# FFN 1's down projection: first four mixer weight tiles split by casting transfers, root table and gain rescale sooner, one low part by an adding transfer

## The chip, the cores and the metric

The kernel runs as one program on one core of a Trainium2 chip. The metric is the device time of one execution in microseconds (us). A core has five engines with instruction queues of their own, each worked off in order: TensorE (PE, matrix products), VectorE (DVE), ScalarE (ACT), GpSimd (POOL) and SyncE (SP, which here only issues transfers). POOL also issues transfers, among them those that add into their destination or change the element type on the way. Transfers run on 16 DMA engines that all queues share. Engines wait for each other by semaphores.

## The reference

One layer of a streaming encoder trunk on 512 tokens of width 1024, in float32:

```
h = x + 0.5 * post1(SwiGLU_1(pre1(x)))            # FFN 1, hidden width 2816
u = pre_mix(h)
[q | k | v | x_rnn | x_gate] = u @ w_in           # the mixer
... RG-LRU branch, windowed attention, gates, merge
h = h + post_mix(merged @ w_o)
y = h + 0.5 * post2(SwiGLU_2(pre2(h)))            # FFN 2
SwiGLU(x) = (silu(x @ w1) * (x @ w3)) @ w2
```

`pre`, `post` and `pre_mix` are root-mean-square norms with a gain vector. The change lies where `@ w2` of FFN 1 ends, its norms `post1` and `pre_mix` are taken, and the first products of the mixer (`x_rnn`, called `xr`) begin.

## The kernel before

**Precision.** Every float32 product is made of three faster ones. An operand is split into a high part (a float32r rounding, names `whi`, `hx`, `Xh`) and a low part (what is left, `wlo`, `hx`, `Xl`), and high by high, high by low and low by high are summed in PSUM. The usual split (`split2`, L226 and L227) is an ACT copy into float32r for the high part and a DVE subtraction for the low one. `split_dma` does without DVE: ACT writes the high part, ACT writes the negated source into the low part, and a POOL transfer adds the source from DRAM to it.

**w2 of FFN 1 by halves.** `Halves` multiplies the hidden activations by `w2` with a scheme of seven products per block pair instead of eight (`m1`, `m5`, `m2`, `m6`, `m3`, `m7`, `m4`, in this order). The inner dimension is cut into six groups (`GS_A`, the last of them half as large), so there are 42 units, numbered u = 0 to 41: product number u // 6, group u % 6. One unit is 12 matmuls of 512 columns (6 in the half group), for two token tiles, into the two PSUM banks of its product (`hw`). `m1`, `m6`, `m7` and `m4` add up in the same banks `bu`, one per token tile: after `m6` and `m7` the partial sums are read out (`out`, into `hc`), and the next product goes on adding on top. So the first `m4` matmul into a bank may not start before the `m7` sum of this bank has been read: that read is the DVE addition at L742.

**What sets the order.** The code is written in the order in which the instructions stand in each queue. `step(u)` first prepares operands up to unit u + 5 (`prep`, two `split2` each: the weight block, then the activations), then runs the hooks of u, then the matmuls. `tok_gemm` with `pre` strings them together: units 0 to 29, `norm(0)` of token tile 0 (rows and `h` by DVE and ACT in turns, L308 to L346), preparation of units 38 and 39, units 30 to 33, units 34 and 35 for tile 0, then for tile 1, `norm(1)`, units 36 to 41 for tile 0, transposes, and so on. `vectors` at u = 18 has POOL load the two gain vectors into all partitions (`bcast`, L294: `bc_ffn1_post_g`, `bc_mix_pre_g`); a hook at u = 24 has ACT rescale the second of them (L438), and a hook at u = 26 has ACT run a tiny reciprocal root so that the root's function table is loaded there (L437).

**The mixer's first tiles.** At u = 26, 28, 31 and 33 (`X_AT`) the raw weight tiles `xr` 0 to 3 are loaded by SP. They are split by `dma_split`, in two parts: part 0 is the ACT high part, part 1 the ACT negated copy and the adding transfer of POOL. Tile 0 is split ahead of `norm(0)`, tile 1 in its middle (`mid`, which stands between the two ACT root steps of a norm), tile 2 ahead of `norm(1)`, tile 3's high part in its middle and its low part after the second transposes.

**Slots.** All large tiles come from one pool of 42 slots of 4 KB per partition. A transfer or an instruction that takes a slot waits until the last reader of the slot's former tile is done.

Of the kernel before, what the change touches and what calls it, by code (L numbers as in the profile page):

```python
# [11 lines left out]
F32R = mybir.dt.float32r  # L12
AF = mybir.ActivationFunctionType
ALU = mybir.AluOpType

P = 128
# [35 lines left out]
def hybrid_layer(ctx: ExitStack, tc: tile.TileContext, a: dict, out: bass.AP):  # L52
# [18 lines left out]
    def small(w, name="m", bufs=4):  # L71
        uid[0] += 1
        return sm.tile([P, w], F32, tag=f"sm{w}", name=f"{name}_{uid[0]}", bufs={1: 11, 4: 12}.get(w, bufs))
# [61 lines left out]
    want("w2b", TAIL_B)  # L135

    st = {"dma": 0, "split": 0, "get": 0}
    raws, pairs, half_split = {}, {}, {}

    loaded = set()  # L140

    def dma_one(k):
        if k not in loaded:
            nm, i = order[k]
            raws[k] = slot([P, D], name=f"raw_{nm}{i}")
            sp.dma_start(out=raws[k], in_=a[nm][i * P : (i + 1) * P, :])
            loaded.add(k)

    def dma_to(n):
        while st["dma"] < min(n, len(order)):  # L150
            dma_one(st["dma"])
            st["dma"] += 1
# [8 lines left out]
        pool.dma_start(out=lo, in_=src, accum_op=ALU.add)  # L161
        return hi, lo

    def dma_split(k, part):
        assert k == st["split"]
        if part == 0:
            dma_to(k + 1)
            half_split[k] = slot([P, D], F32R, name="whi"), slot([P, D], F32R, name="wlo")
            act.activation(half_split[k][0], raws[k], AF.Copy)
            return  # L170
        pairs[k] = hi, lo = half_split.pop(k)
        act.activation(lo, raws.pop(k), AF.Copy, scale=-1.0)
        nm, i = order[k]
        pool.dma_start(out=lo, in_=a[nm][i * P : (i + 1) * P, :], accum_op=ALU.add)
        st["split"] += 1
# [202 lines left out]
    def tok_gemm(nm, xs, n, R, gpost_name, scale, gpre_name, first, x_to=None, xf=None, spill=False, then=None, eps=None, pre=None):  # L378
# [52 lines left out]
        def norm(t, mid=None):  # L431
            us[t] = norms(acc[t], t, g[0], scale, g[1], spill, ep(t), mid, pre and pre.part(t), (1, 0) if pre and t > 1 else (0, 1))

        if pre:
            G = pre.G
            pre.hooks[3 * G].append(vectors)
            pre.hooks[4 * G + 2].append(lambda: act.activation(small(1, "tiny"), veps[:, 0:1], AF.Abs_reciprocal_sqrt))  # L437
            pre.hooks[4 * G].append(lambda: act.activation(g[1], g[1], AF.Copy, scale=NEWT))  # L438
            x0 = st["get"] + len(tail)
            for i, u in enumerate(X_AT):  # L440
                pre.hooks[u].append(lambda i=i: dma_to(x0 + i + 1))

            def x_split(i, parts=(0, 1)):
                for p in parts:
                    dma_split(x0 + i, p)

            for u in range(5 * G):
                pre.step(u)
            for t in range(2):
                acc[t] = [pre.bank["bc"][t], pre.bank["bx"][t]]  # L450
            pre.prep(5 * G + LEAD + 3)
            x_split(0)
            norm(0, lambda: x_split(1))
            pre.prep(7 * G - 2)
            for u in range(5 * G, 6 * G - 2):
                pre.step(u)
            for t in range(2):
                for u in range(6 * G - 2, 6 * G):
                    pre.step(u, (t,))
                if t == 0:  # L460
                    pre.prep(7 * G)
            for t in range(2, 4):
                acc[t] = [pre.bank["bu"][t - 2], None]
            pre.hid.eo.clear()
            x_split(2)
            norm(1, lambda: x_split(3, (0,)))
            for u in range(6 * G, 7 * G):
                pre.step(u, (0,))
            trs[0] = transpose_mm(us[0])
            transpose_out(trs[0], 0)  # L470
            for u in range(6 * G, 6 * G + 2):
                pre.step(u, (1,))
            trs[1] = transpose_mm(us[1])
            transpose_out(trs[1], 1)
            x_split(3, (1,))
            norm(2, lambda: [transpose_xf(trs[0], 0, xf), transpose_xf(trs[1], 1, xf, (0,))])
            transpose_xf(trs[1], 1, xf, (1,))
            for u in range(6 * G + 2, 7 * G):
                pre.step(u, (1,))
            pre.bank.clear()  # L480
        else:
# [121 lines left out]
    class Halves:  # L603
# [84 lines left out]
        def prep(self, n, load=True):  # L688

            G = self.G  # L690
            while self.ready < min(n, self.cap):
                u = self.ready
                self.ready += 1
                m, i = self.names[u // G], u % G
                J = len(self.gs[i])
                if load:
                    self.load(max(G, u))
                b, odd, half = self.OPERANDS[m]
                hi = slot([P, 2, 512], F32R, name="whi")
                if J == 2:  # L700
                    lo = slot([P, 2, 512], F32R, name="wlo")
                else:
                    hi, lo = hi[:, 0:1, :], hi[:, 1:2, :]
                if u < U_SLOTS or u >= self.in_slots:
                    xs = slot([P, 2, 2, 256], F32R, name="hx")
                else:
                    xs = uT[:, :, (u + 1) % 8, :].rearrange("p e (j c) -> p e j c", j=2)
                src = self.again.pop(i) if m == "m3" else self.raw[b, i]
                split2(hi, lo, src)
                split2(xs[:, 0, :J, :], xs[:, 1, :J, :], self.x(i, odd, half))  # L710
                self.ops[u] = hi, lo, xs
                if self.again_at <= u < self.again_at + G:
                    n = u - self.again_at
                    self.again[n] = slot([P, 2, 512], name=f"raw_{self.nm}")[:, : len(self.gs[n]), :]
                    sp.dma_start(out=self.again[n], in_=self.src("b22", n))
                self.sums(m, i)
# [1133 lines left out]
GRAW_AT = (29, 30)  # L1850
TB_AT = (34, 35, 36, 37)

BY_DMA = {("wg", i) for i in range(2)} | {("xr", i) for i in range(4)}

BY_POOL = {("wg", i) for i in range(2, 8)} | {("wk", 0), ("wk", 1)}

TAIL_A = ()
LEAD = 5
# [72 lines left out]
```

## Time and profile before

| | us |
|---|---|
| runs shown (3) | 1104.5, 1101.29, 1103.9; median 1103.9 |
| the profiled execution, its own time | 1103.1 |
| its span, first to last instruction | 1100.9 |
| PE busy in the span | 1089.4 (99%) |
| DVE busy | 937.1 (85%) |
| ACT busy | 711.2 (65%) |
| POOL busy | 423.8 (38%) |

Times inside the execution are counted from the span's start. A row of the timeline reads: start, duration, engine, line, operation, output <- input, shapes, count; in brackets at its end the idle time of the engine just before it and what ended it. Durations of ACT and DVE overlap a little: the next instruction starts about 0.1 us before the one before it is listed as ended. PE matmuls are pipelined; what counts there is the distance between starts (0.227 us for 512 columns at full clock). Tile names are printed without buffer numbers, so the group's `bc_ffn1_post_g` reads `bc_ffn_post_g`. The end of FFN 1's `w2` that the change touches lies between 280 and 355 us.

### The profile page before, as it was taken

To read this page: it belongs to the slowest core of one execution; us is meant where nothing else is said; L and a number is where in the kernel's file an instruction comes from. 1 tells how busy PE (TensorE), PEld (TensorE's weight loads), DVE (VectorE), ACT (ScalarE), POOL (GpSimd) and SP (SyncE) were. 2 spreads that over 40 slices of the span, in tenths; PEclk is the share of its full clock that TensorE was granted. 3 is DMA by queue.
4 is the path that set the end of the run, shared out by engine and by line. 5 is a ranking of instruction groups with operands and counts; after the bars stand their busy time and mean duration, and the time that the engine had idled before them with its cause. 6 is when DMAs were issued, how large, how long until landed. Compare 5 with 4: busy or idle time off the path is not lost.

```text
span 1100.9 us, 18128 instructions
## 1 busy us (share of the span) xinstructions
PE 1089.4 (99%) x6850; PEld 986.1 (90%) x6850; DVE 937.1 (85%) x1347; ACT 711.2 (65%) x1243; POOL 423.8 (38%) x351
## 2 busy tenths in 40 slices
PE   9999999999989999999999999999999999999997
PEld 7899999998879877999888888888999999998886
DVE  5898999999997998888678867767789989889996
ACT  7756555598777778756656664456555555578872
POOL 0144833232101623233557574010877656633200
PEclk9999999999999999999999999999999999999999
DMA  9325663399957753146222245342423323449923
GB/s 343 118 79 143 142 138 113 108 201 213 241 172 204 186 131 99 40 161 247 71 78 95 96 154 210 134 185 78 140 77 116 102 91 103 148 105 239 206 81 134
DMA packets 54615, 157.51 MB, mean 143 GB/s; under 512 B 5616, under 2 KB 7536, under 8 KB 54528
## 3 DMA queue, kind: packets, MB, share of 16 engines
q1 hardware_dynamic: 41136, 124.85, 33.5%
q0 software_dynamic: 13104, 30.98, 15.5%
q8 instruction: 54, 0.88, 0.3%
q10 hardware_dynamic: 288, 0.52, 0.2%
q14 instruction: 33, 0.27, 0.1%
HBM read 140.61 MB, written 13.62 MB: 140 GB/s over the span
## 4 chain that ended last, share of the span: by engine, by line
PE 70%; ACT 1%; DVE 1%; DMA 0%; issue 0%; DVEq 0%; ACTq 0%
PE f L237 9%; PE f L239 9%; PE f L238 9%; PE c L843 8%; PE c L842 8%; PE c L841 8%; PE hw L730 4%; PE hw L732 4%; PE hw L731 4%; PE acc L257 1%; PE acc L255 1%; PE acc L256 1%; PE pt L1694 1%; PE s L1658 1%; PE s L1657 1%; PE tr L355 1%
## 5 line engine op out<-in xcount | busy, mean ns | idle before, releaser
L842 PE MATMUL c<-uT,wlo 128*128 128x256 f32 x516 | 146.0, 283 | 0.0
L843 PE MATMUL c<-uT,whi 128*128 128x256 f32 x516 | 146.0, 283 | 0.0
L841 PE MATMUL c<-uT,whi 128*128 128x256 f32 x516 | 146.0, 283 | 0.0
L841 PE MATMUL c<-Xh,whi 128*128 128x256 f32 x504 | 142.7, 283 | 0.0
L842 PE MATMUL c<-Xh,wlo 128*128 128x256 f32 x504 | 142.6, 283 | 0.0
L237 PE MATMUL f<-uT,whi 128*128 128x512 f32 (+1 forms) x380 | 138.6, 365 | 0.0
L238 PE MATMUL f<-uT,wlo 128*128 128x512 f32 (+1 forms) x380 | 136.9, 360 | 0.0
L239 PE MATMUL f<-uT,whi 128*128 128x512 f32 (+1 forms) x380 | 136.9, 360 | 0.0
L843 PE MATMUL c<-Xl,whi 128*128 128x256 f32 x456 | 129.1, 283 | 0.0
L227 DVE TENSOR_TENSOR wlo<-S,whi 128x1024 fp32r<-128x1024 f32 x86 | 116.7, 1357 | 6.4 <-ACT whi L226 3.2
L226 ACT ACTIVATE whi<-S 128x1024 fp32r<-128x1024 f32 x86 | 88.5, 1054 | 36.3 <-DVE S L890 35.2
L842 PEld LDWEIGHTS c<-uT,wlo 128*128 128x128 f32 x516 | 99.0, 192 | 0.2
L841 PEld LDWEIGHTS c<-uT,whi 128*128 128x128 f32 x516 | 99.0, 192 | 0.2
L843 PEld LDWEIGHTS c<-uT,whi 128*128 128x128 f32 x516 | 99.0, 192 | 0.0
L841 PEld LDWEIGHTS c<-Xh,whi 128*128 128x128 f32 x504 | 96.8, 192 | 0.3 <-issue 0.3
L842 PEld LDWEIGHTS c<-Xh,wlo 128*128 128x128 f32 x504 | 96.8, 192 | 0.0
L730 PE MATMUL hw<-whi,uT 128*128 128x512 f32 x240 | 93.4, 389 | 0.0
L732 PE MATMUL hw<-whi,uT 128*128 128x512 f32 x240 | 93.4, 389 | 0.0
L843 PEld LDWEIGHTS c<-Xl,whi 128*128 128x128 f32 x456 | 87.5, 192 | 0.0
L731 PE MATMUL hw<-wlo,uT 128*128 128x512 f32 x216 | 84.0, 389 | 0.0
L237 PEld LDWEIGHTS f<-uT,whi 128*128 128x128 f32 x380 | 71.7, 189 | 12.1 <-issue 1.4
L239 PEld LDWEIGHTS f<-uT,whi 128*128 128x128 f32 x380 | 71.7, 189 | 11.0
(419 smaller groups left out, 3221.7 us busy)
## 6 DMA issues: line engine op xcount, KB each, us to landing
raw_w1b<-in_w1b_dram SPq DMA_DIRECT2D x22, 512.0 KB, 4.1
raw_w3b<-in_w3b_dram SPq DMA_DIRECT2D x22, 512.0 KB, 4.4
raw_w3a<-in_w3a_dram SPq DMA_DIRECT2D x21, 512.0 KB, 4.5
raw_w1a<-in_w1a_dram SPq DMA_DIRECT2D x20, 512.0 KB, 4.1
raw_wg<-in_wg_dram SPq DMA_DIRECT2D x16, 512.0 KB, 3.9
raw_w2a<-in_w2a_dram SPq DMA_DIRECT2D x15, 512.0 KB, 6.9
raw_w2a<-in_w2a_dram POOLq DMA_DIRECT2D x15, 512.0 KB, 9.9
raw_w2b<-in_w2b_dram SPq DMA_DIRECT2D x15, 512.0 KB, 5.9
```

The source lines that it names most:

```text
L226: act.activation(hi, src, AF.Copy)
L227: dve.tensor_tensor(out=lo, in0=src, in1=f32(hi), op=ALU.subtract)
L237: pe.matmul(ps[:, c0:c1], wh[:, s], h_, start=k == 0 and c0 == 0, stop=False, skip_group_check=True)
L238: pe.matmul(ps[:, c0:c1], wl[:, s], h_, start=False, stop=False, skip_group_check=True)
L239: pe.matmul(ps[:, c0:c1], wh[:, s], l_, start=False, stop=k == KT - 1, skip_group_check=True)
L255: pe.matmul(acc[n], x[:, 0, c], wh[:, s], start=first, stop=False, skip_group_check=skip)
L730: pe.matmul(ps, xs[:, 0, j, c], hi[:, j, :], start=start and j == 0, stop=False, skip_group_check=True)
L731: pe.matmul(ps, xs[:, 0, j, c], lo[:, j, :], start=False, stop=False, skip_group_check=True)
L732: pe.matmul(ps, xs[:, 1, j, c], hi[:, j, :], start=False, stop=i == self.G - 1, skip_group_check=True)
L841: pe.matmul(ps, wh[:, s], xh, start=first, stop=False, skip_group_check=True)
L842: pe.matmul(ps, wl[:, s], xh, start=False, stop=False, skip_group_check=True)
L843: pe.matmul(ps, wh[:, s], xl, start=False, stop=k == 3, skip_group_check=True)
```

## The change

- `xr` 0 to 3 are no longer loaded raw by SP. A POOL transfer (L147 of the changed kernel) reads them from DRAM and writes the float32r high part `whi` itself. ACT's high-part copies go away; ACT's negated copy (L172) now reads `whi`, and the adding transfer stays. One slot per tile is used where there were two.
- These negated copies stand one place later than the old splits: tile 0 in the middle of `norm(0)`, tile 1 after the preparation of units 38 and 39, tile 2 in the middle of `norm(1)`, tile 3 after the second transposes.
- The tiny root (with the table load) moves from u = 26 to u = 19, the rescale of `bc_mix_pre_g` from u = 24 to u = 22.
- Unit 33 (`m7`, group 3) gets its weight's low part as an ACT negated copy and a POOL transfer that adds the raw block out of its slot (L707 to L709); DVE's subtraction goes away.
- Of the last `m4` preparations, unit 40 stands between the two `m7` sums of DVE, unit 41 behind the second; before, both stood between them.

```
@@ dma_one
+            if order[k] in BY_CAST:
+                raws[k] = slot([P, D], F32R, name="whi")
+                pool.dma_start(out=raws[k], in_=a[nm][i * P : (i + 1) * P, :])
+            else:
+                raws[k] = slot([P, D], name=f"raw_{nm}{i}")
+                sp.dma_start(out=raws[k], in_=a[nm][i * P : (i + 1) * P, :])
@@ dma_split -> cast_split
+    def cast_split(k):
         assert k == st["split"]
+        dma_to(k + 1)
+        pairs[k] = hi, lo = raws.pop(k), slot([P, D], F32R, name="wlo")
+        act.activation(lo, f32(hi), AF.Copy, scale=-1.0)
         nm, i = order[k]
         pool.dma_start(out=lo, in_=a[nm][i * P : (i + 1) * P, :], accum_op=ALU.add)
@@ tok_gemm
-            pre.hooks[4 * G + 2].append(lambda: act.activation(small(1, "tiny"), veps[:, 0:1], AF.Abs_reciprocal_sqrt))
-            pre.hooks[4 * G].append(lambda: act.activation(g[1], g[1], AF.Copy, scale=NEWT))
+            pre.hooks[3 * G + 1].append(lambda: act.activation(small(1, "tiny"), veps[:, 0:1], AF.Abs_reciprocal_sqrt))
+            pre.hooks[3 * G + 4].append(lambda: act.activation(g[1], g[1], AF.Copy, scale=NEWT))
...
-            x_split(0)
-            norm(0, lambda: x_split(1))
+            norm(0, lambda: x_split(0))
             pre.prep(7 * G - 2)
+            x_split(1)
             for u in range(5 * G, 6 * G - 2):
                 pre.step(u)
             for t in range(2):
                 for u in range(6 * G - 2, 6 * G):
                     pre.step(u, (t,))
-                if t == 0:
-                    pre.prep(7 * G)
+                pre.prep(7 * G - 1 + t)
...
-            x_split(2)
-            norm(1, lambda: x_split(3, (0,)))
+            norm(1, lambda: x_split(2))
...
-            x_split(3, (1,))
+            x_split(3)
@@ Halves.prep
-                split2(hi, lo, src)
+                if (self.nm, m, i) in BY_ADD:
+                    act.activation(hi, src, AF.Copy)
+                    act.activation(lo, f32(hi), AF.Copy, scale=-1.0)
+                    pool.dma_start(out=lo, in_=src, accum_op=ALU.add)
+                else:
+                    split2(hi, lo, src)
@@ tables
-BY_DMA = {("wg", i) for i in range(2)} | {("xr", i) for i in range(4)}
+BY_DMA = {("wg", i) for i in range(2)}
+BY_CAST = {("xr", i) for i in range(4)}
+BY_ADD = {("w2a", "m7", 3)}
```

In the following rows the numbers behind a name count the buffers of the program; `hEO` is the hidden activation, `raw_w2a` a raw block of `w2`, `hc` a read-out partial sum. First ACT, around the rescale and the table load, before the change:

```order
L226 ACTIVATE whi_512_3368<-raw_w2a_497_3268 128x1024
L226 ACTIVATE uT_78<-hEO_292_1845 128x512
L226 ACTIVATE whi_514_3386<-raw_w2a_501_3286 128x1024
L226 ACTIVATE uT_78<-hEO_358_2347 128x512
L744 ACTIVATE hc_517_3398<-hw_440_2900 128x512
L744 ACTIVATE hc_517_3398<-hw_441_2901 128x512
L226 ACTIVATE whi_518_3401<-raw_w2a_506_3313 128x1024
L226 ACTIVATE uT_78<-hEO_104_483 128x512
L438 ACTIVATE bc_mix_pre_g_504_3294<-bc_mix_pre_g_504_3294 128x1024
L226 ACTIVATE whi_520_3420<-raw_w2a_509_3336 128x512
```

The same place of ACT's queue after the change:

```order
L437 ACT_TABLE_LOAD
L437 ACTIVATE tiny_507_3318<-veps_75 128x1
L226 ACTIVATE whi_508_3332<-raw_w2a_489_3220 128x1024
L226 ACTIVATE uT_78<-hEO_152_791 128x512
L226 ACTIVATE whi_511_3352<-raw_w2a_493_3244 128x1024
L226 ACTIVATE uT_78<-hEO_226_1324 128x512
L226 ACTIVATE whi_513_3370<-raw_w2a_497_3268 128x1024
L226 ACTIVATE uT_78<-hEO_292_1845 128x512
L438 ACTIVATE bc_mix_pre_g_504_3294<-bc_mix_pre_g_504_3294 128x1024
L226 ACTIVATE whi_515_3389<-raw_w2a_501_3286 128x1024
L226 ACTIVATE uT_78<-hEO_358_2347 128x512
L746 ACTIVATE hc_518_3401<-hw_440_2900 128x512
```

The rescale now stands right behind unit 27's activations; the preparation of unit 28, the two read-outs `hc` and unit 29 have moved from ahead of it to behind it, and the table load from behind it to three units ahead of it.

Then POOL's queue from the gain vectors on, before:

```order
L294 DMA bc_mix_pre_g_504_3294<-in_mix_pre_g_dram 128x1024
L652 DMA raw_w2a_418_2753<-in_w2a_dram 128x512
L174 DMA wlo_543_3537<-in_xr_dram 128x1024
L174 DMA wlo_556_3564<-in_xr_dram 128x1024
L174 DMA wlo_582_3694<-in_xr_dram 128x1024
L174 DMA wlo_595_3721<-in_xr_dram 128x1024
```

And after:

```order
L294 DMA bc_mix_pre_g_504_3294<-in_mix_pre_g_dram 128x1024
L649 DMA raw_w2a_418_2753<-in_w2a_dram 128x512
L147 DMA whi_524_3445<-in_xr_dram 128x1024
L147 DMA whi_530_3485<-in_xr_dram 128x1024
L709 DMA wlo_532_3500<-raw_w2a_410_2728 128x1024
L174 DMA wlo_553_3559<-in_xr_dram 128x1024
L174 DMA wlo_565_3594<-in_xr_dram 128x1024
L147 DMA whi_567_3611<-in_xr_dram 128x1024
L147 DMA whi_569_3639<-in_xr_dram 128x1024
L174 DMA wlo_590_3712<-in_xr_dram 128x1024
```

Five transfers are new in POOL's queue; the casting loads of tiles 2 and 3 stand behind the adding transfer of tile 1, which waits for ACT's negated copy of that tile.

Last DVE's queue around the two `m7` sums (L742 before, L744 after), before:

```order
L227 TENSOR_TENSOR hx_567_3595<-hEO_358_2347,hx_567_3595 128x512
L742 TENSOR_TENSOR hc_478_3148<-hw_440_2900,hc_478_3148 128x512
L227 TENSOR_TENSOR wlo_575_3669<-raw_w2a_502_3289,whi_574_3668 128x1024
L227 TENSOR_TENSOR hx_576_3670<-hEO_104_483,hx_576_3670 128x512
L227 TENSOR_TENSOR whi_577_3675<-raw_w2a_418_2753,whi_577_3675 128x512
L227 TENSOR_TENSOR hx_578_3676<-hEO_163_838,hx_578_3676 128x256
L742 TENSOR_TENSOR hc_478_3148<-hw_441_2901,hc_478_3148 128x512
```

And after:

```order
L227 TENSOR_TENSOR hx_564_3589<-hEO_358_2347,hx_564_3589 128x512
L744 TENSOR_TENSOR hc_478_3148<-hw_440_2900,hc_478_3148 128x512
L227 TENSOR_TENSOR wlo_573_3666<-raw_w2a_502_3289,whi_572_3665 128x1024
L227 TENSOR_TENSOR hx_574_3667<-hEO_104_483,hx_574_3667 128x512
L744 TENSOR_TENSOR hc_478_3148<-hw_441_2901,hc_478_3148 128x512
L227 TENSOR_TENSOR whi_577_3684<-raw_w2a_418_2753,whi_577_3684 128x512
L227 TENSOR_TENSOR hx_578_3685<-hEO_163_838,hx_578_3685 128x256
```

The first `m7` sum stands behind the preparation of units 38 and 39 in both; the second has moved ahead of unit 41's two subtractions.

More of the change, by code (lines that the diff above doesn't have):

```diff
@@ L137, in hybrid_layer @@
     st = {"dma": 0, "split": 0, "get": 0}
-    raws, pairs, half_split = {}, {}, {}
+    raws, pairs = {}, {}
     loaded = set()
@@ L144, in dma_one @@
             nm, i = order[k]
-            raws[k] = slot([P, D], name=f"raw_{nm}{i}")
-            sp.dma_start(out=raws[k], in_=a[nm][i * P : (i + 1) * P, :])
+            if order[k] in BY_CAST:
[4 more added lines that the diff above has]
+                sp.dma_start(out=raws[k], in_=a[nm][i * P : (i + 1) * P, :])
             loaded.add(k)
@@ L162, in split_dma @@
         return hi, lo
-    def dma_split(k, part):
+    def cast_split(k):
         assert k == st["split"]
[L166 to L172, printed above, removed]
+        dma_to(k + 1)
+        pairs[k] = hi, lo = raws.pop(k), slot([P, D], F32R, name="wlo")
+        act.activation(lo, f32(hi), AF.Copy, scale=-1.0)
         nm, i = order[k]
@@ L441, in tok_gemm, with x_split @@
                 pre.hooks[u].append(lambda i=i: dma_to(x0 + i + 1))
-            def x_split(i, parts=(0, 1)):
-                for p in parts:
-                    dma_split(x0 + i, p)
+            def x_split(i):
+                cast_split(x0 + i)
             for u in range(5 * G):
```

## Prediction

> **What bounds the kernel now.** I read the busy shares first, then PE's waits, then the timelines of PE, DVE, ACT and POOL from 280 to 345 us.
>
> ```profile
> PE 1089.4 (99%) x6850; PEld 986.1 (90%) x6850; DVE 937.1 (85%) x1347; ACT 711.2 (65%) x1243; POOL 423.8 (38%) x351
> PE hw L730 <- ACT hx L226: 2.9, 1, 2.9
> ```
>
> PE is busy for all but 11.5 us of the span, and its waits hold one of any size, 2.9 us at a matmul of `Halves`. The change removes no matmul, so all it can gain is this wait and what follows from it.
>
> ```profile
> 321.78 0.39 PE L732 MATMUL hw<-whi,uT 128*128 128x512 f32 x1
> 325.07 0.47 PE L730 MATMUL hw<-whi,hx 128*128 128x512 f32 x1 [2.90 <-ACT hx L226]
> 329.49 0.39 PE L730 MATMUL hw<-whi,hx 128*128 128x512 f32 x1
> 325.67:329.08 3.41, 3.41 (x10) 2.67 (x9) 3.38 (x7) 2.21 (x3) 0.23 (x1) 0.50 1.04 423
> ```
>
> PE stands from 322.17 to 325.07 ahead of the first `m4` matmul. The last row (a window: PE, PEld, DVE, ACT and POOL busy, granted clock, DMA share, GB/s) shows that the clock is 0.50 for 3.41 us afterwards. Half of that is lost, 1.7 us. The stall costs 4.6 us in all, 0.42% of 1103.
>
> The releaser named is not the true one: the `hx` in question is unit 41's, and unit 36 doesn't need it. What the first `m4` matmul must wait for is the read-out of its bank, DVE's first `m7` sum at L742:
>
> ```profile
> 310.85 0.68 DVE L227 TENSOR_TENSOR hx<-hEO,hx 128x512 fp32r<-128x512 f32 x1
> 311.46 0.68 DVE L308 TENSOR_TENSOR hc<-hw,hc 128x512 f32<-128x512 f32 x1
> 320.75 1.23 DVE L227 TENSOR_TENSOR wlo<-raw_w2a,whi 128x1024 fp32r<-128x1024 f32 x1 [1.01 <-ACT whi L226]
> 324.24 0.69 DVE L742 TENSOR_TENSOR hc<-hw,hc 128x512 f32<-128x512 f32 x1
> ```
>
> It ends at 324.93, just ahead of PE's 325.07. In DVE's queue it stands behind units 38 and 39 (from 320.75), these behind `norm(0)` (from L308 at 311.46), and that behind unit 37 (to 311.53). So whatever delays units 28 to 37 on ACT or DVE, or lengthens `norm(0)`, delays PE one for one.
>
> ```profile
> 282.54 1.06 ACT L226 ACTIVATE whi<-raw_w2a 128x1024 fp32r<-128x1024 f32 x1 [1.90 <-PE hw L731]
> 288.94 0.61 ACT L226 ACTIVATE uT<-hEO 128x512 fp32r<-128x512 f32 x1
> 289.46 1.05 ACT L226 ACTIVATE whi<-raw_w2a 128x1024 fp32r<-128x1024 f32 x1
> 291.60 1.28 ACT L744 ACTIVATE hc<-hw 128x512 f32<-128x512 f32 x2 [0.57 <-PE hw L732]
> 294.25 1.05 ACT L438 ACTIVATE bc_mix_pre_g<-bc_mix_pre_g 128x1024 f32<-128x1024 f32 x1
> 297.61 1.28 ACT L437 ACT_TABLE_LOAD   x1
> 299.01 1.04 ACT L226 ACTIVATE whi<-raw_w2a 128x1024 fp32r<-128x1024 f32 x1
> 308.14 0.61 ACT L226 ACTIVATE hx<-hEO 128x512 fp32r<-128x512 f32 x1
> 308.66 1.05 ACT L169 ACTIVATE whi<-raw_xr 128x1024 fp32r<-128x1024 f32 x1
> 312.23 0.63 ACT L310 ACTIVATE junk<-hc 128x512 f32<-128x512 f32 x1 [1.58 <-DVE hc L308]
> 314.79 1.04 ACT L169 ACTIVATE whi<-raw_xr 128x1024 fp32r<-128x1024 f32 x1
> 316.69 0.61 ACT L334 ACTIVATE junk<-h 128x512 f32<-128x512 f32 x1
> 319.68 1.04 ACT L226 ACTIVATE whi<-raw_w2a 128x1024 fp32r<-128x1024 f32 x1
> 331.45 1.04 ACT L169 ACTIVATE whi<-raw_xr 128x1024 fp32r<-128x1024 f32 x1
> 280.66 0.58 POOL L294 DMA_DIRECT2D bc_mix_pre_g<-in_mix_pre_g_dram  x1
> bc_mix_pre_g<-in_mix_pre_g_dram POOLq DMA_DIRECT2D x1, 512.0 KB, 12.7
> 285.00:295.00 10.00, 10.00 (x45) 8.28 (x45) 9.34 (x12) 7.95 (x11) 0.00 (x0) 1.00 1.08 314
> ```
>
> ACT has no pause from 291.60 to the end of unit 37's `hx` (308.75). `bc_mix_pre_g` is issued at 280.66 and takes 12.7 us to land: it is there at 293.4. The rescale of it, L438, ran at 294.25 and so never waited.
>
> **The change part by part.**
>
> *The rescale two units earlier.* This decides. After the change L438 stands right behind unit 27's `uT`, the row at 288.94, so ACT reaches it at 289.46. Nothing ahead of it in POOL's queue or on the DMA engines changes, so the transfer still lands at 293.4, and ACT, which works in order, waits 4.0 us there with units 28 to 37 queued behind it. Of this 0.57 us is no loss, since ACT would have waited for PE at 291.60 anyway. Cost to ACT: 4.0 - 0.57 = 3.4 us. Bounds: none, were the vector there by 289.5 (a landing in 8.8 us); and 1 us more for each us that it lands later. I keep 12.7, because the DMA share of 285 to 295 is 1.08, full, and those transfers are the same.
>
> *The table load sooner.* Between the `uT` of 296.97 and the `whi` at 299.01 it takes 1.5 us of ACT's time (297.51 to 299.01). At its new place, behind the copies that end at 280.6, ACT had 1.90 us idle before 282.54, waiting for PE; the load and the tiny root fit. Gain to ACT: 1.5 us, new cost nothing; without that cover it would only shift units that again wait for PE.
>
> *Unit 33's low part by adding.* ACT gains one negated copy, priced like the copies in these rows: +1.05 us. DVE loses one subtraction of 1.23. The adding transfer is issued near 306, and unit 33's matmuls stand about 315.4 (units 34 and 35, two tiles, are 18 matmuls of 0.227 before 322.17, unit 33 twelve before that). It has 9 us. The nearest row, four adding transfers out of SBUF, gives 4.9; the slowest row, 12.7, would cost 3 us. I take 4.9, hidden.
>
> ```profile
> wlo<-xf POOLq DMA_DIRECT2D x4, 512.0 KB, 4.9
> ```
>
> *ACT up to unit 37:* +3.4 - 1.5 + 1.05 = +3.0 us, so it ends at 311.7 instead of 308.75. DVE had some of it in hand: it ended unit 37 at 311.53, 2.8 behind ACT. With ACT late, DVE runs close behind instead. Following the last units through: ACT gives unit 36's `whi` near 309.7 and unit 37's near 311.2; DVE, about 1.7 us per unit as in 308 to 311.5, has been waiting for ACT since unit 34 and ends unit 37 at 313.5. That is +2.0. Bounds: +1.8, ACT's delay less the subtraction that DVE is spared (3.0 - 1.2), and +3.0, if it follows ACT in full.
>
> *`xr` 0 to 3 by casting.* Ahead of `norm(0)` ACT is spared two copies that stood in its idle time (1.58 before 312.23): nothing. In its middle ACT made two copies of `xr` 1 (314.79 to 316.69) and now one of `xr` 0; the squares at 316.69 then wait for DVE's `h` instead. Gain 0.3 us. Tile 1's copy now stands behind unit 39 and ahead of unit 40, off the way to the first `m7` sum. The casting loads of tiles 0 and 1 wait on POOL for the slots that SP's loads waited for, the later at 300.44; behind them stands only unit 33's adding transfer near 306, and both land long before ACT reads them at about 316.7 and 324.2, at the far end of 12.7 us too. SP is relieved of four issues. Tile 3's load is read near 339.5, 12 us after its issue: nothing.
>
> ```profile
> 300.44 0.33 SPq L146 DMA_DIRECT2D raw_xr<-in_xr_dram  x1
> ```
>
> *The second `m7` sum ahead of unit 41* takes 1.0 us off that sum. It is needed by tile 1's `m4` units and `norm(1)` later; PE is then inside tile 0's, so nothing by itself.
>
> So the first `m7` sum and PE start 2.0 - 0.3 = 1.7 us later: **PE stands 4.6 us instead of 2.9**, resuming near 326.8. If the clock comes back at the same 329.08, 2.3 us of half clock are left and cost 1.1 instead of 1.7: -0.6. Bounds of this term: -1.7 (none) and 0 (the whole 3.41 us again). I take -0.6, the reading of the one row there is. The Trainium skill, TensorE: Matmul & The Clock Gate, Part 1, has this as a free-running window of about 3.4 us, after an idle one of which the clock is halved; the 3.41 us row agrees, and by that page the stretch after the wait may in another execution come out at up to its full 1.7 us, estimated as half of one window.
>
> *Tile 2's casting load.* It is the one new wait that can be late. On POOL it stands behind tile 1's adding transfer, which waits for ACT's negated copy behind unit 39: about 325.2. So it is issued near 326.2, where SP used to issue the load at 317.8. ACT needs it in the middle of `norm(1)`, where the copy at 331.45 stood, now about 333.0. Behind it are `norm(1)`'s squares and the transposes of tile 1:
>
> ```profile
> 335.23 0.75 DVE L345 SCALAR_TENSOR_TENSOR hg<-h,r,bc_mix_pre_g 128x512 f32<-128x512 f32 x1
> 337.87 1.03 PE L355 MATMUL tr<-ident,hg 128*128 128x128 f32 x8
> raw_xr<-in_xr_dram SPq DMA_DIRECT2D x1, 512.0 KB, 3.6
> raw_xr<-in_xr_dram SPq DMA_DIRECT2D x1, 512.0 KB, 8.6
> wlo<-in_xr_dram POOLq DMA_DIRECT2D x1, 512.0 KB, 9.1
> ```
>
> `hg` was ready 1.9 us before PE took it. With `hg` 1.7 later and PE 1.1 later, 1.3 us are left. So a landing within 6.8 us costs nothing at all, up to 8.1 nothing to PE, and each us more costs PE one. No casting transfer is in the trace. The nearest rows are the same tile's loads: 3.6 us on empty DMA engines, 8.6 in this stretch, and the 9.1 of the adding transfer beside it; the far end is 12.7. That is 0 to +4.6; I take 8.6, so +0.5, since the four loads of `h` share the engines as before. The Trainium skill, DMA: Bandwidth & Descriptors, Anatomy of one DMA, gives a transfer issued by POOL 2.0 us and its bytes at 436 GB/s, for 512 KB an estimate of 3.2 us. By it this term would be 0 and the sum +1.1; the rows of POOL here, 4.9 to 12.7, disagree, and they decide.
>
> **Sum.** +1.7 - 0.6 + 0.5 = +1.6 us on the profiled execution's 1103.1, whose span is 1100.9; it stands 0.8 under the median of 1103.9. So 1105.5 in terms of the median.
>
> **The rivals.**
>
> *Tile 2's load is late in earnest* (POOL's queue takes the place of the first wait). If a cast costs the DMA engines what `bc_mix_pre_g` took, 12.7 us, PE waits 4.6 us more at the transposes of tile 1: +1.7 - 0.6 + 4.6 = +5.7, 1109.6. From a landing in 10.3 us on the sum passes 0.3%. For it: two POOL transfers back to back with an adding one ahead. Against: the DMA share falls to 0.54 from 330 on:
>
> ```profile
> 330.00:345.00 15.00, 15.00 (x82) 12.85 (x81) 11.71 (x27) 11.31 (x26) 3.68 (x5) 1.00 0.54 115
> ```
>
> *The gain vector is there in time* (faster). Without the 4.0 us wait ACT ends unit 37 one us sooner than before (-1.5 + 1.05 - 0.57) and DVE, one subtraction lighter, 1.1 sooner; with the 0.3 of `norm(0)` PE stands only 1.5 us. If the clock then stays up, that is -1.4 - 1.7 = -3.1: 1100.8. It decides from a landing under 8.8 us. Against it: the 12.7 and the full DMA engines.
>
> *The change doesn't reach PE*: were the true releaser something other than the L742 sum, the stall would stay 2.9 and the time 1103.9. Against it: 324.93 to 325.07.
>
> **How the numbers follow.** Forecast (ACT waits at the rescale, PE 4 to 5 us, tile 2 at most 2 us late; its own range 1104 to 1107) 0.60; tile 2 late in earnest or another new wait 0.24; gain vector in time 0.10; no effect 0.06. 0.3%, 3.3 us, is about what a measurement can tell from no change; the three runs alone spread by 3.2 us. Slower takes the second case and a tenth of the first, less what of the second stays under 3.3: 0.27. Faster takes half of the third with its scatter: 0.06. Same: 0.67. The range reaches from the third case's inner half, 1101.5, to just under the second's far end, 1109.0.
>
> **What would show it.** The change's profile should show ACT idle some 4 us ahead of L438, released by POOL's `bc_mix_pre_g`; no idle time from the table load at its new place; unit 37's `hx` on DVE ending near 313.5; the first `m7` sum near 326 and PE's wait at 4.6; PE not waiting for unit 33's low part. A PE wait ahead of the transposes of tile 1 would be the second case; a PE wait under 2 us, or L438 not waiting, would make the prediction wrong.

## The result and the profile after

The change costs a little. In eleven executions each, run side by side, the changed kernel has a median of 1105.4 us (1104.08 to 1105.99) and the kernel before 1102.89 us (1100.93 to 1104.5). The ratio is 1.0024, with a 95% interval of 1.0014 to 1.0033. That is inside the 0.3% that the prediction counted as the same, at its slower end. The profiled execution of the changed kernel took 1104.66 us (span 1102.7), 1.56 more than the profiled one of before.

Engine shares and PE's largest wait, from the page and the waits of the changed kernel:

```profile
PE 1089.6 (99%) x6850; PEld 986.2 (89%) x6850; DVE 936.6 (85%) x1346; ACT 708.4 (64%) x1240; POOL 426.7 (39%) x356
PE hw L732 <- DVE hc L744: 4.3, 1, 4.3
```

PE has the same work and the same single wait as before, now 4.3 us long instead of 2.9. This time the profile names the true releaser, DVE's first `m7` sum (L744). PE's timeline of the changed kernel around the wait, and the window behind it (columns as in the prediction):

```profile
321.62 0.39 PE L734 MATMUL hw<-whi,uT 128*128 128x512 f32 x1
326.28 0.47 PE L732 MATMUL hw<-whi,hx 128*128 128x512 f32 x1 [4.27 <-DVE hc L744]
326.74:330.16 3.42, 3.42 (x10) 2.65 (x9) 3.38 (x7) 0.54 (x3) 0.39 (x1) 0.50 1.00 339
```

PE resumes 1.21 us later than before (326.28 against 325.07), though its wait has grown by 1.37, because this execution stands 0.16 us ahead where PE stops (321.62 against 321.78). Then PE runs a whole 3.42 us at half clock, as it did before. Its last matmul is 1.18 us later (1094.81 against 1093.63), so what was lost at the wait is neither recovered nor added to. The span grows by 1.8; the 0.6 us between that and 1.2 lie behind the last matmul and aren't explained here. Over all twelve profiles of this study this last piece takes 7.3 to 8.0 us.

ACT of the changed kernel: the table load at its new place, then the rescale L438, then the last copy before `norm(0)`:

```profile
280.49 1.28 ACT L437 ACT_TABLE_LOAD   x1
282.38 1.06 ACT L226 ACTIVATE whi<-raw_w2a 128x1024 fp32r<-128x1024 f32 x1 [0.39 <-PE hw L733]
288.79 0.61 ACT L226 ACTIVATE uT<-hEO 128x512 fp32r<-128x512 f32 x1
293.13 1.06 ACT L438 ACTIVATE bc_mix_pre_g<-bc_mix_pre_g 128x1024 f32<-128x1024 f32 x1 [3.73 <-DMA bc_mix_pre_g<-in_mix_pre_g_dram]
310.51 0.61 ACT L226 ACTIVATE hx<-hEO 128x512 fp32r<-128x512 f32 x1
```

ACT waits 3.73 us for the gain vector, and the unit behind the table load still waits 0.39 for PE, so the load costs nothing there. ACT ends unit 37 at 311.12, 2.4 us later than before. The transfer itself, from the DMA view of the changed kernel, with the adding one of unit 33:

```profile
bc_mix_pre_g<-in_mix_pre_g_dram POOLq DMA_DIRECT2D x1, 512.0 KB, 12.6
wlo<-raw_w2a POOLq DMA_DIRECT2D x1, 512.0 KB, 4.4
```

DVE of the changed kernel, from its wait for ACT to the first `m7` sum:

```profile
295.17 1.23 DVE L227 TENSOR_TENSOR wlo<-raw_w2a,whi 128x1024 fp32r<-128x1024 f32 x1 [3.87 <-ACT whi L226]
312.42 0.68 DVE L227 TENSOR_TENSOR hx<-hEO,hx 128x512 fp32r<-128x512 f32 x1
313.03 0.68 DVE L308 TENSOR_TENSOR hc<-hw,hc 128x512 f32<-128x512 f32 x1
321.97 1.23 DVE L227 TENSOR_TENSOR wlo<-raw_w2a,whi 128x1024 fp32r<-128x1024 f32 x1 [1.02 <-ACT whi L226]
325.45 0.68 DVE L744 TENSOR_TENSOR hc<-hw,hc 128x512 f32<-128x512 f32 x1
```

DVE inherits ACT's wait (3.87 us at 295.17). It starts `norm(0)` 1.57 us later than before (313.03 against 311.46), comes out of it 1.22 later (321.97 against 320.75), and ends the first `m7` sum 1.2 later (326.13 against 324.93).

POOL's issues, ACT's copy and DVE's last `hg` of tile 1, and PE's transposes of it:

```profile
325.70 1.43 POOL L147 DMA_DIRECT2D whi<-in_xr_dram  x2
334.52 1.06 ACT L172 ACTIVATE wlo<-whi 128x1024 fp32r<-128x1024 f32 x1 [1.82 <-DMA whi<-in_xr_dram]
337.76 0.75 DVE L345 SCALAR_TENSOR_TENSOR hg<-h,r,bc_mix_pre_g 128x512 f32<-128x512 f32 x1
339.09 1.03 PE L355 MATMUL tr<-ident,hg 128*128 128x128 f32 x8
```

POOL's row is a pair, the casting loads of tiles 2 and 3. Tile 2's is late: ACT waits 1.82 us for it. But `hg` is done at 338.51, and PE comes to the transposes at 339.09, so PE doesn't wait.

### The profile page after: what moved, and what is told of

Same layout as the page of the kernel before. It is cut to its first block, busy times and chain, and to the rows that moved or that the text cites. A ratio compares the mean times of both kernels' runs of the same rounds, so it can differ in the third digit from the quotient of the medians.

```text
span 1102.7 us, 18128 instructions
## 1 busy us (share of the span) xinstructions
PE 1089.6 (99%) x6850; PEld 986.2 (89%) x6850; DVE 936.6 (85%) x1346; ACT 708.4 (64%) x1240; POOL 426.7 (39%) x356
## 4 chain that ended last, share of the span: by engine, by line
PE 98%; DVE 1%; issue 0%; DMA 0%; ACT 0%; DVEq 0%; ACTq 0%
PE c L843 13%; PE c L845 13%; PE c L844 13%; PE f L237 10%; PE f L238 9%; PE f L239 9%; PE hw L732 6%; PE hw L733 6%; PE hw L734 6%; PE acc L257 1%; PE acc L255 1%; PE acc L256 1%; PE pt L1696 1%; PE s L1660 1%; PE s L1659 1%; PE tr L355 1%
```

## The experiments

The theory is the prediction's: the rescale makes ACT wait for the gain vector, the wait goes through DVE's unit 37 and `norm(0)` to the first `m7` sum, and PE starts later by it. Rivals: the transfers added to POOL's queue (the casting loads) make the loss, or the extra copy and transfer of unit 33 do, or the wait at L438 never reaches PE. Each kernel is the changed kernel or the kernel before with the lines shown. In the expectations and here, times are medians, and ratios are against the kernel before on the same chip, with 95% intervals.

### The rescale back at its old place

```
@@ changed kernel
-            pre.hooks[3 * G + 4].append(lambda: act.activation(g[1], g[1], AF.Copy, scale=NEWT))
+            pre.hooks[4 * G].append(lambda: act.activation(g[1], g[1], AF.Copy, scale=NEWT))
```

> The changed kernel with the rescale of bc_mix_pre_g back at u = 24, all else kept. Theory (ACT's wait of 3.7 us at the rescale is what costs): ACT waits for no transfer ahead of it, PE's wait ahead of the first m4 matmul falls from 4.3 to about 1.4 us, and the time lies 1 to 3 us under the kernel before, the 3 if the half clock goes away too. Rival 1 (tile 2's casting load on POOL costs): PE's first wait stays above 2.9 us or a wait of 2 us and more stands ahead of tile 1's transposes, time at or above the kernel before. Rival 2 (unit 33's extra ACT copy costs): PE's first wait falls to no less than 2.9 us, time about 1 us above the kernel before.

Measured: 1101.14 us, ratio 0.9982 (0.9974 to 0.9991). One line turns the loss into a gain. PE's waits and the rescale on ACT in this kernel:

```profile
PE hw L732 <- DVE hc L744: 1.3, 1, 1.3
PE tr L355 <- DVE hg L345: 1.2, 1, 1.2
293.84 1.05 ACT L438 ACTIVATE bc_mix_pre_g<-bc_mix_pre_g 128x1024 f32<-128x1024 f32 x1
```

L438 runs at 293.84 without a wait. From there on all is 3.2 us sooner than in the changed kernel, step by step: ACT's end of unit 37 (307.92 against 311.12), DVE's start of `norm(0)` (309.83 against 313.03), PE's first `m4` matmul (323.08 against 326.28). These three rows, two windows of PE's clock, and tile 2's copy and transposes:

```profile
307.31 0.61 ACT L226 ACTIVATE hx<-hEO 128x512 fp32r<-128x512 f32 x1
309.83 0.68 DVE L308 TENSOR_TENSOR hc<-hw,hc 128x512 f32<-128x512 f32 x1
323.08 0.47 PE L732 MATMUL hw<-whi,hx 128*128 128x512 f32 x1 [1.32 <-DVE hc L744]
322.00:326.00 4.00, 2.92 (x13) 2.47 (x14) 4.00 (x7) 1.97 (x4) 1.95 (x3) 1.00 0.99 394
326.00:330.00 4.00, 4.00 (x20) 3.30 (x19) 3.65 (x9) 1.75 (x5) 0.00 (x0) 1.00 1.06 268
331.61 1.06 ACT L172 ACTIVATE wlo<-whi 128x1024 fp32r<-128x1024 f32 x1 [2.11 <-DMA whi<-in_xr_dram]
335.66 1.09 PE L355 MATMUL tr<-ident,hg 128*128 128x128 f32 x8 [1.24 <-DVE hg L345]
```

The windows show full clock after the 1.3 us wait. So 2.95 us of wait and an estimated 1.7 of half clock (half of the 3.42 us stretch) are saved. Of this 1.24 us is lost again at the transposes: PE now gets there soon enough to meet tile 2's late casting load. 2.95 + 1.7 - 1.24 is 3.4; the two profiled executions differ by 3.5.

### The earlier rescale alone

```
@@ kernel before
-            pre.hooks[4 * G].append(lambda: act.activation(g[1], g[1], AF.Copy, scale=NEWT))
+            pre.hooks[3 * G + 4].append(lambda: act.activation(g[1], g[1], AF.Copy, scale=NEWT))
```

> The kernel before with one edit, the rescale at u = 22 instead of u = 24. Theory: ACT waits about 4 us at the rescale, and with no table load moved away PE's first wait grows from 2.9 to about 5.6 us, time 2.5 to 4 us above the kernel before. Rivals 1 and 2: none of their parts is in this kernel, so PE's wait stays at 2.9 us and the time within 1 us of the kernel before.

Measured: 1106.47 us, ratio 1.0029 (1.0017 to 1.0042), worse than the whole change. Its waits, and its rescale:

```profile
PE hw L730 <- ACT hx L226: 5.9, 1, 5.9
293.43 1.06 ACT L438 ACTIVATE bc_mix_pre_g<-bc_mix_pre_g 128x1024 f32<-128x1024 f32 x1 [3.75 <-DMA bc_mix_pre_g<-in_mix_pre_g_dram]
```

No casting transfer and no adding one of unit 33 is in this kernel, and PE waits 3.0 us more than before. ACT's 3.75 less the 0.57 that it would have waited for PE is 3.2: nearly all of it arrives. PE's resumption, and windows of 4 us around it:

```profile
328.16 0.76 PE L730 MATMUL hw<-whi,hx 128*128 128x512 f32 x1 [5.87 <-ACT hx L226]
322.00:326.00 4.00, 0.29 (x2) 0.00 (x0) 2.96 (x5) 3.85 (x6) 0.00 (x0) 0.79 0.88 220
326.00:330.00 4.00, 1.84 (x4) 1.49 (x5) 4.00 (x6) 2.50 (x5) 0.00 (x0) 0.50 1.02 331
330.00:334.00 4.00, 4.00 (x17) 3.28 (x16) 3.80 (x8) 2.75 (x5) 0.85 (x1) 0.86 1.12 398
```

The clock is at half for (0.21 + 0.50 + 0.14) x 4 / 0.5, 6.8 us, but this stretch begins at 324.3, while PE still stands. Only its last 3.0 us, from 328.16 to 331.12, meet matmuls.

### The earlier table load alone

```
@@ kernel before
-            pre.hooks[4 * G + 2].append(lambda: act.activation(small(1, "tiny"), veps[:, 0:1], AF.Abs_reciprocal_sqrt))
+            pre.hooks[3 * G + 1].append(lambda: act.activation(small(1, "tiny"), veps[:, 0:1], AF.Abs_reciprocal_sqrt))
```

> The kernel before with one edit, the root's table load at u = 19 instead of u = 26. Theory: it fits into ACT's idle 1.9 us there and takes 1.5 us out of ACT's busy stretch, of which DVE gets back the 1.16 us that it waited behind the load: PE's first wait 1.6 to 1.8 us, time 1 to 3 us under the kernel before, 3 if the half clock goes away. Rival (the load was covered by DVE's own work): PE's wait stays at 2.9 us, no change of time.

Measured: 1100.14 us, ratio 0.9976 (0.9968 to 0.9985). The wait and the stretch behind it:

```profile
PE hw L730 <- ACT hx L226: 1.6, 1, 1.6
325.60:329.00 3.40, 3.36 (x15) 2.83 (x16) 3.40 (x6) 1.93 (x2) 0.00 (x0) 1.00 1.02 405
```

The wait is 1.3 us shorter and no half clock follows. The profile is of an execution of 1102.21 us; nine of the eleven took 1099.8 to 1100.3, and what sets the other two apart lies at the start of the program (last section). 1.3 + 1.7 is 3.0; the medians differ by 2.8 (1102.97 against 1100.14). This is the good part of the change.

### The casting loads alone

The kernel before with `BY_CAST`, `cast_split` and the new places of the splits, and with nothing else of the change; `BY_ADD` is empty, and the second `m7` sum, the table load and the rescale stand as before:

```
@@ kernel before
-BY_DMA = {("wg", i) for i in range(2)} | {("xr", i) for i in range(4)}
+BY_DMA = {("wg", i) for i in range(2)}
+BY_CAST = {("xr", i) for i in range(4)}
+BY_ADD = set()
```

> The kernel before with the casting transfers for xr 0 to 3 and their negated copies in the changed places alone; rescale, table load, unit 33 and the second m7 sum as before. Theory: PE's first wait 2.6 us (0.3 less by the copy spared inside norm(0)), tile 2's load lands about 8.3 us after its issue and is hidden by the half clock or costs PE up to 1 us ahead of tile 1's transposes; time within 1 us of the kernel before. Rival 1 (the casting loads cost): 2 us and more above the kernel before, by a PE wait ahead of the transposes.

Measured: 1102.94 us, ratio 1.0003 (0.9994 to 1.0012). The wait, ACT's copy of tile 2, and PE's transposes:

```profile
PE hw L733 <- DVE hc L745: 2.5, 1, 2.5
333.20 1.06 ACT L172 ACTIVATE wlo<-whi 128x1024 fp32r<-128x1024 f32 x1 [1.96 <-DMA whi<-in_xr_dram]
337.69 1.03 PE L355 MATMUL tr<-ident,hg 128*128 128x128 f32 x8
```

The wait is 0.4 shorter than before, near the 0.3 us that the prediction gave `norm(0)`. Tile 2 is 1.96 us late, and again PE doesn't feel it behind a half-clock stretch. The casting loads do not make the loss. But none of these eleven executions is shorter than 1102.18, while 27 of 93 of the kernel before take 1100.8 to 1101.5 (see below): a cost of about 1 us where the half clock stays away, like the 1.24 with the rescale back, fits; no trace of such an execution was taken.

### The rescale one unit earlier than before

```
@@ changed kernel
-            pre.hooks[3 * G + 4].append(lambda: act.activation(g[1], g[1], AF.Copy, scale=NEWT))
+            pre.hooks[3 * G + 5].append(lambda: act.activation(g[1], g[1], AF.Copy, scale=NEWT))
```

> The changed kernel with the rescale one unit later, at u = 23 instead of u = 22 (u = 24 gave a PE wait of 1.3 us, u = 22 one of 4.3). Theory: ACT then waits for bc_mix_pre_g with one unit's preparation less queued behind it, about 1.5 us less harm: PE's first wait about 2.9 us, between the two. The time lies between the two kernels, about 1103. If instead the position counted only as before or after the landing at 293.1, it would be at 1.3 or at 4.3 us.

Measured: 1102.8 us (1102.21 to 1105.27), ratio 1.0005 (0.9997 to 1.0014). This is u = 23, one unit earlier than in the kernel before and one later than in the changed kernel.

```profile
PE hw L732 <- DVE hc L744: 2.8, 1, 2.8
292.79 1.06 ACT L438 ACTIVATE bc_mix_pre_g<-bc_mix_pre_g 128x1024 f32<-128x1024 f32 x1 [2.26 <-DMA bc_mix_pre_g<-in_mix_pre_g_dram]
```

With this the three places of the rescale make a row: ACT waits 0, 2.26 and 3.73 us, PE 1.3, 2.8 and 4.3. The vector takes 12.6 us from issue to landing in all three, and lands at about 293.

### Unit 33 by subtraction again

```
@@ changed kernel
-BY_ADD = {("w2a", "m7", 3)}
+BY_ADD = set()
```

> The changed kernel with unit 33's low part by DVE's subtraction again. If the extra ACT copy (1.05 us) is the dearer side, PE's first wait falls below 4.3 us by up to 1; if DVE's subtraction (1.23) is, it grows. Theory: DVE runs close behind ACT there, both shift nearly alike: 4.3 to 4.6 us, time within 0.5 us of the changed kernel.

Measured: 1105.8 us, ratio 1.0025 (1.0016 to 1.0034), like the changed kernel. PE's wait and the clock behind it, in windows of 4 us:

```profile
PE hw L732 <- DVE hc L744: 4.6, 1, 4.6
322.00:326.00 4.00, 0.00 (x0) 0.00 (x0) 3.91 (x5) 4.00 (x7) 0.72 (x2) 0.87 1.01 340
326.00:330.00 4.00, 3.60 (x9) 2.86 (x10) 4.00 (x7) 1.28 (x3) 1.27 (x3) 0.50 1.03 373
330.00:334.00 4.00, 4.00 (x15) 3.22 (x14) 3.62 (x9) 1.74 (x5) 0.00 (x0) 0.77 1.08 313
```

The adding transfer is worth 0.3 us of the wait; in the medians it doesn't show. The clock here is at half for (0.13 + 0.50 + 0.23) x 4 / 0.5, 6.9 us, twice the stretch of the changed kernel's profile. By the first row it begins near 325.0, while PE still stands; PE resumes at 326.40 and runs 5.4 us of it. That loses 2.7 us by half, against 1.7 in the changed kernel's profile, and the two profiled executions differ by 1.0 (1105.64 against 1104.66).

### The second `m7` sum back behind unit 41

```
@@ changed kernel
-                pre.prep(7 * G - 1 + t)
+                if t == 0:
+                    pre.prep(7 * G)
```

> The changed kernel with the second m7 sum back behind both last m4 preparations. Theory: PE is inside tile 0's units when it is needed, so no wait changes: PE's first wait 4.3 us, time that of the changed kernel, within 0.5 us. Rival (the earlier second sum helped by up to 1 us): about 1 us slower, with a later norm(1) and a PE wait ahead of tile 1's transposes.

Measured: 1105.37 us, ratio 1.0032 (1.002 to 1.0044).

```profile
PE hw L733 <- DVE hc L745: 4.3, 1, 4.3
```

The move of the second sum does nothing that can be measured.

### The kernel before once more

No edit: the kernel before against itself, to see how its own executions scatter.

> The kernel before, unchanged, for the granted clock of each of its executions. Its runs fall into a group near 1101.2 and one of 1102.9 to 1104.5. Theory: the 2.9 us wait sometimes does and sometimes doesn't bring the half clock of 3.41 us, which costs 1.7 us; then the short executions show a mean clock about 0.0015 higher than the long ones. Rival (the two groups differ in something else): no relation of time and clock.

Measured: 1102.78 us, ratio 1.0001 (0.9992 to 1.0009). All 93 executions of the kernel before in this study fall into three groups: 27 at 1100.8 to 1101.5, 49 at 1102.4 to 1103.5, 17 at 1103.9 to 1104.7. The groups' medians are 1101.2, 1102.9 and 1104.2, about 1.7 and 1.4 apart; half of one 3.41 us stretch is 1.7. The mean clock listed is 0.998 for the first group and 0.996 or 0.997 for the other two. Two profiles of the middle group are at hand (1103.1 and 1102.78), both with one half-clock stretch after a 2.9 us wait. In the second of them:

```profile
324.91 0.47 PE L730 MATMUL hw<-whi,hx 128*128 128x512 f32 x1 [2.90 <-ACT hx L226]
326.14 0.61 PE L732 MATMUL hw<-whi,hx 128*128 128x512 f32 x1
```

Here five matmuls run at full clock after the same wait, and the half clock begins at 326.14, 1.23 us behind PE's resumption; in the first profile it began 0.60 behind it (325.67 and 325.07). So where the stretch falls isn't set by the wait alone. That the first group lacks this stretch fits, but no trace of that group was taken.

### The rescale on POOL

```
@@ changed kernel
-            pre.hooks[3 * G + 4].append(lambda: act.activation(g[1], g[1], AF.Copy, scale=NEWT))
+            pre.hooks[4 * G + 5].append(lambda: pool.tensor_scalar(out=g[1], in0=g[1], scalar1=NEWT, scalar2=None, op0=ALU.mult))
```

> The changed kernel with the rescale done by POOL at u = 29, behind its second casting load, instead of by ACT at u = 22. Theory: no ACT wait and one ACT instruction of 1.05 us less, so PE's first wait is 0.4 to 0.8 us and the clock stays up; tile 2's casting load, no longer hidden by a half clock, then costs PE about 1 us ahead of tile 1's transposes as in the first experiment (1.2). Time about 1100.3, some 0.8 under that experiment's 1101.1. If the rescale on POOL holds up its transfers, the wait ahead of the transposes is longer than 1.2.

Measured: 1100.55 us, ratio 0.9982 (0.9973 to 0.9991). The waits, POOL's rescale, and the DVE subtraction beside it:

```profile
PE hw L732 <- DVE hc L744: 1.0, 1, 1.0
PE tr L355 <- DVE hg L345: 0.8, 1, 0.8
302.97 2.78 POOL L438 TENSOR_SCALAR bc_mix_pre_g<-bc_mix_pre_g 128x1024 f32<-128x1024 f32 x1
303.21 1.87 DVE L227 TENSOR_TENSOR wlo<-raw_w2a,whi 128x1024 fp32r<-128x1024 f32 x1 [0.26 <-PE hw L734]
```

The time is as expected, PE's wait is longer than the 0.4 to 0.8 expected. ACT is rid of the rescale, 1.05 us, but the wait falls from the 1.3 of the old place only to 1.0. The subtraction beside POOL's operation takes 0.65 us longer (1.87 against 1.22): counted from the issue of the gain vector it starts 0.95 us sooner than with the rescale at its old place and ends 0.3 sooner, and DVE is on the path.

### The good parts together

The kernel before, with the earlier table load, the rescale on POOL and unit 33 by adding; `xr` 0 to 3 are loaded by SP and split by ACT as before:

```
@@ kernel before
-            pre.hooks[4 * G + 2].append(lambda: act.activation(small(1, "tiny"), veps[:, 0:1], AF.Abs_reciprocal_sqrt))
-            pre.hooks[4 * G].append(lambda: act.activation(g[1], g[1], AF.Copy, scale=NEWT))
+            pre.hooks[3 * G + 1].append(lambda: act.activation(small(1, "tiny"), veps[:, 0:1], AF.Abs_reciprocal_sqrt))
+            pre.hooks[4 * G + 5].append(lambda: pool.tensor_scalar(out=g[1], in0=g[1], scalar1=NEWT, scalar2=None, op0=ALU.mult))
...
+BY_ADD = {("w2a", "m7", 3)}
```

> The kernel before with the table load at u = 19, the rescale by POOL at u = 29 and unit 33's low part by adding; xr 0 to 3 loaded by SP and split as before. Theory: the parts that helped, without tile 2's casting load: PE's first wait 0.7 to 1.1 us, none ahead of the transposes, clock full, time 1099 to 1100, under the 1100.1 of the table load alone. If the POOL rescale or the adding transfer gives back what it takes off ACT, the time is that of the table load alone or above.

Measured: 1099.64 us (1099.53 to 1100.1), ratio 0.9971 (0.996 to 0.9983). It beats both kernels.

```profile
PE hw L735 <- ACT hx L226: 1.3, 1, 1.3
```

The time is as expected, the wait of 1.3 us isn't (0.7 to 1.1). It is more than the 1.0 with the casting loads, since `norm(0)` is again about as long as before (9.24 us against 8.92 with them); in exchange PE waits for nothing at the transposes. From the table load alone (0.9976) the interval doesn't tell it apart.

## Why the prediction was right, point by point

- *The rescale makes ACT wait, and this decides.* Shown: with the rescale back the loss is gone (0.9982), the rescale alone makes it (1.0029), and the place in between gives a wait in between. The wait was 3.73 us against 4.0; the vector landed at 293.1 rather than 293.4.
- *The table load is free at its new place.* Shown: in the changed kernel ACT still waits 0.39 for PE behind it, and the load alone gains 0.24%.
- *ACT's unit 37 3.0 us later, DVE's 2.0.* The direction is right, the sizes were too large: +2.4 on ACT (311.12) and +1.6 on DVE (313.10 against 313.5). 0.3 of ACT's error is the earlier landing.
- *`norm(0)` 0.3 shorter.* It is: from L308 to unit 38's subtraction 8.94 us against 9.29 before.
- *PE's wait 4.6, resuming near 326.8.* It was 4.3, resuming at 326.28. The term of +1.7 measured +1.4 by the wait and +1.2 by the resumption (0.16 is this trace's lead); the difference is nearly all the 0.4 too much in DVE's unit 37.
- *0.6 us of half clock saved.* This term failed. The prediction took it that full clock would come back at the same instant as before, 329.08. It came back at 330.16, after PE had run a whole stretch of 3.42 us at half clock; the right value in this trace was its bound of 0. But the stretch isn't counted from PE's resumption either: the traces put its two ends on steps of 3.41 us whose place differs from execution to execution (last section), so this term has no one value for a kernel. In the profile with unit 33 by subtraction, where PE resumed only 0.12 us later, the clock was at half for two stretches. The seven of eleven executions of the changed kernel that took 1105.0 to 1106.0 have a mean clock of 0.995, the four from 1104.1 to 1104.8 one of 0.996; the two profiles here with two stretches list 0.995 as well. That a second stretch makes these seven longer is argued, not shown.
- *Tile 2's casting load, +0.5.* Its landing was sized well: issued in the pair that begins at 325.70 and read at 334.52, at most 8.8 us against 8.6. Its cost to PE was 0. PE came to the transposes 1.2 us later than before, against 1.1 forecast; what differed was `hg`, done 2.5 us later than before (338.51 against 335.98) and not 3.5, the forecast's 1.7 + 1.8. Half of that one us is the copy itself: before, ACT idled 0.42 us behind it, waiting for DVE's `h`, and the late copy finds `h` done (the squares follow the copy's start by 0.97 us instead of 1.47). The other half is that `norm(1)` starts 1.2 us later than before (329.32 against 328.11) and not 1.7. With the rescale back, where PE has no half-clock stretch, the same load costs 1.24. The Trainium skill, DMA: Bandwidth & Descriptors, Anatomy of one DMA, would have had it land in an estimated 3.2 us; the four casting loads here took 3.8 to 9.5 us with a median of 7.6, the gain vector 12.6, so its fit doesn't hold where the DMA engines are full.
- *Unit 33 by adding: hidden.* Right: the transfer took 4.4 us against the 4.9 taken, PE never waits for it, and without it the time is the same.
- *The second `m7` sum: nothing.* Right, 1105.37 without it.

The sum in the trace is +1.2 + 0 + 0 = +1.2 to the last matmul and +1.56 in the execution's own time, against +1.6 forecast. Three terms were off: the half clock by 0.6 too little, PE's start and tile 2 by 0.5 too much each. That these nearly cancel, and that the unexplained piece behind the last matmul fills the gap, is luck. So is the closeness of 1105.5 to the median of 1105.4: the forecast started from 1103.9, the median of three executions of the kernel before; over eleven that median is 1102.9, so between the medians the change costs 2.5, not 1.6. What the prediction had right is the mechanism: which instruction waits, for what, and by which way the wait reaches PE. Of the rivals, *the gain vector there in time* is what the kernel with the rescale put back shows: 1100.8 was forecast for it and 1101.14 measured, with a wait of 1.3 instead of 1.5 and full clock as forecast, and 1.24 us at the transposes that the rival had not counted. Here too the base helps: the gain forecast was 3.1, between the medians it is 1.8 (3.1 with the 1.24 added). *Tile 2 late in earnest* fell with the 8.8 us of its load, and *the change doesn't reach PE* with the releaser L744, now named at 4.27 us.

## What to carry to other kernels

Before an instruction that reads a transfer is moved forward, compare its new start with the landing of the transfer, and then ask who is queued behind it: here a rescale of 1 us, moved by two units, held an engine for 3.7 us, and the wait came out, by way of a third engine, on one that never touches the vector. Move a function's table load into idle time of its engine instead; that alone was worth 0.24%. And when a stall of the matrix engine is shortened, look at what it had been covering: a casting load that cost nothing behind the stall cost 1.2 us once the stall was gone.

## What the runs showed of the hardware

- The granted clock changes only at steps of 3.413 us, and where the steps lie differs from execution to execution. In each of the twelve profiles every later change stands a whole number of steps behind the trace's first clock record, where full clock begins: 325.67 - 4.82 is 94 steps (the kernel before), 326.14 - 5.28 is 94 (its second profile), 326.74 - 5.89 is 94 (the changed kernel), 324.29 - 6.85 is 93 (the rescale alone).
- In these traces the clock of a step goes with PE's idle time in the step before it (PE's stop taken as its resumption less the listed wait). From full clock, steps with 2.0, 2.2, 2.5 and 2.8 to 3.3 us idle were followed by half clock, steps with 1.3 or less were not; at half clock, a step with 1.4 us idle kept it (unit 33 by subtraction), one with 0.5 ended it (the rescale alone). So in the profiles waits of 1.0, 1.3, 1.3 and 1.6 us brought no half clock, waits of 2.5, 2.8, 2.9 and 4.3 us one step, waits of 4.6 and 5.9 two, which began inside the wait. Shortening the wait from 2.9 to 1.6 was worth 2.8 us between the medians; lengthening it from 2.9 to 4.3 cost 1.2 us at PE's last matmul and 2.5 between the medians. An estimate from these rows: a wait of 2.9 us that a step's end cuts into two parts of under 2.0 brings no half clock; if the steps lie anywhere with equal chance, that is up to (2 x 2.0 - 2.9) / 3.41, a third of all executions, and the short group of the kernel before is 27 of 93. The Trainium skill, TensorE: Matmul & The Clock Gate, Part 1, puts the lower clock behind at least one idle window of about 3.4 us, and has these windows run free of the kernel's start; length and free running agree, but here 2.0 us of idle time in one step were enough.
- Half clock can also stand at the start of the program, and the listed clock doesn't show it there. In the profiled execution of the earlier table load alone, one of two among its eleven at 1102.2 instead of about 1100, the first real matmuls are 0.43 us apart instead of 0.23, while the granted clock is listed as 1.00. The trace has no clock record ahead of 10.31 us, where the distance falls to 0.23 (the first records of the other profiles stand at 4.1 to 7.0), and without a record 1.00 is listed:

```profile
7.28 0.63 PE L1201 MATMUL f<-uT,whi 128*128 128x512 f32 x1
7.70 0.63 PE L1202 MATMUL f<-uT,wlo 128*128 128x512 f32 x1
```

All that follows stands 1.9 us later in this trace (the last `m7` matmul at 323.68 against 321.78 before). This may be what makes the third group of the kernel before; no trace of that group shows it.
- A rescale of 128x1024 took POOL 2.78 us where ACT takes 1.05, and a DVE subtraction beside it 1.87 instead of 1.22; with the good parts together the two rows are 2.77 and 1.88. The Trainium skill, GPSIMD Engine Reference, 1. Specifications, says that GpSimd shares its SBUF interfaces with VectorE and that instructions of two SBUF inputs contend; the row agrees.
